# Seven-product matrix blocks run in an interleaved order, with other pauses in two heads

## The chip, the cores and the metric

The kernel runs on one core of a Trainium2 chip. The metric is the device time of one execution in microseconds (us); of several executions the median is given. A profile of one execution records every instruction of the engines: TensorE (PE; PEld is its loading of weights), VectorE (DVE), ScalarE (ACT), GpSimd (POOL) and SyncE (SP), which here only issues DMAs.

## What is computed

Two layers of a bidirectional encoder on a sequence of 512 rows with 2048 features, all in 32-bit floats: an attention layer (16 query heads, 4 key/value heads, rotary positions, gate) and a retention layer (8 heads, forward and backward decay, gate), each followed by a residual sum and a layer norm. Cut to what matters here:

```python
def attention_mixer(h, w_in, q_gain, k_gain, w_out, cos, sin):
    q, k, v, g = jnp.split(h @ w_in, ...)             # 2048 x 5120
    ...
    return (o * jax.nn.silu(g)) @ w_out

def retention_mixer(h, w_in, decay_exp, w_out, cos, sin):
    q, k, v, g = jnp.split(h @ w_in, ...)             # 2048 x 12288
    ...
    o = head_group_norm(fwd + bwd).reshape(B, S, R_V_WIDTH)
    return (o * jax.nn.silu(g)) @ w_out               # 4096 x 2048

def reference(x, ...):
    for i in range(DEPTH):
        y = attention_mixer(x, ...) if i % 2 == 0 else retention_mixer(x, ...)
        x = layer_norm(ALPHA * x + y, ln_gain[i], ln_bias[i])
    return x
```

## The kernel before

**Split products.** Every 32-bit matrix is split into a high and a low part (`split`, L107: a copy by ScalarE, L109, and a subtraction by VectorE, L110), and a product is made of three matmuls: high by high, high by low, low by high (`mm3`, lines 227 to 229). One such group of three is counted as 0.68 us (`MM3`).

**Blocks of seven products.** The input projections of both layers and the output projection of the retention layer's first six heads use a scheme of the Strassen kind: a weight block of 1024 columns is cut in four quarters (`q11`, `q12`, `q21`, `q22`), and seven products of quarter size, numbered 1 to 7, do the work of eight. A product runs over `nc` chunks of weights (four in the layers, two in the pairs); a chunk is 128 x 1024 numbers (512 KB), and for each chunk PE does four groups of three matmuls, two for either half of the rows. Products accumulate in three sets of two PSUM banks, named by `CHAIN`: x takes 1, 6, 7 and 4 one after another, y takes 5 and 3, z takes 2. After each product the two banks are read out by `spill` (L343 copies after 1, 5 and 6; L346 subtracts after 3, L350 after 7, L354 adds after 2; after 4 the consumer reads), and the next product on the same set can't start before that. The eight banks are shared with the heads' scores, values and transposes.

**Where the quarters come from.** `Block.fetch`, `make` and `follow` load a chunk as raw data (SP, L117), add to it in place by an accumulating DMA (POOL, `onto`, L121) or by VectorE (L155 for product 6, L157 for product 4), and split it. A block that is not "first" loads q11 for product 1, adds q12 behind it for product 5, adds q22 (loaded for 6) on VectorE, and q21 (loaded for 2) on VectorE for 4; q22 + q12 makes product 7. A "first" block takes product 2 early: it loads q11 for product 1, q21 for product 2, then q11 again with q12 added for 5, and after 6 adds q21 by DMA. Raw chunks lie in nine buffers (`rp`), which the heads' loads share; split chunks in three (`wp`). The split of a chunk is made two chunks before its use (`AHEAD`), and it needs the `wp` buffer of three chunks earlier.

**Order.** PE's instructions run in the program's order; those of the other engines are placed by a scheduler. The order of products is `ORDER` or, for "first" blocks, `FIRST`:

```python
ORDER = (1, 5, 6, 3, 7, 2, 4)
FIRST = (1, 2, 5, 6, 3, 7, 4)
```

In either layer the blocks 0 and 1 are "first": 1 and 2 of block 0, 1 and 2 of block 1, then 5, 6, 3, 7, 4 of block 0, the same of block 1, then the other blocks in `ORDER` (`in_stream`). The retention output has three pairs of heads; each pair has two blocks of two chunks, the first in `FIRST`, the second in `ORDER` (`out_pair`), and its results are added to a tensor in DRAM (`yD2`). The same lists give the order in which chunks are fetched.

**Heads.** The eight retention heads (`Head.run`) are interleaved with a stream of such products: four score units (`s_unit`, one for each 128 keys), four value units (`o_unit`, each followed by a normalisation on VectorE, POOL and ScalarE, L946 to L950), and transposes of their results (`o_close`, L462). Between them `work.pump(each)` puts `each` us of products into PE's order: 15 units a head, 1.4 us each for heads 0 and 1, which run beside the last input block, and 2.5 us for the others, two of which run beside each pair. `Head.open` loads and splits what head 0 needs.

Of the kernel before, what the change touches and what calls it, by code (L numbers as in the profile page):

```python
# [16 lines left out]
NT = S // P  # L17
# [14 lines left out]
AHEAD = 2  # L32
FETCH = 3
MM3 = 0.68
LOOK = 2
A_KEEP, R_KEEP = 2, 0

PAIRS = 3

ORDER = (1, 5, 6, 3, 7, 2, 4)  # L40
FIRST = (1, 2, 5, 6, 3, 7, 4)
CHAIN = {1: "x", 6: "x", 7: "x", 4: "x", 5: "y", 3: "y", 2: "z"}


# [1 line left out]
def encoder_trunk_kernel(  # L46
# [184 lines left out]
    class Stream:  # L231
# [14 lines left out]
        def until(self, done):  # L246
            while not done():
                self.pump(MM3)

# [64 lines left out]
    def products(blk, op, seq, evacuate):  # L314
        for p in seq:
            ch, fresh = CHAIN[p], p in (1, 5, 2)
            if fresh:
                blk.bk[ch] = [bank() for _ in range(2)]
            for c in range(blk.nc):
                ks = next_chunk()  # L320
                for hook in blk.hooks.get((p, c), ()):
                    hook()
                run_later()
                for j in range(2):
                    k = 2 * c + j
                    for t in range(2):
                        mm3(blk.bk[ch][t], op.st(p, k, t), ks[j], fresh and k == 0, k == 2 * blk.nc - 1, not fresh)
                        yield MM3
            evacuate(blk, p)
# [4 lines left out]
    def spill(deliver):  # L334

        def evacuate(blk, p):
            keep, bk = blk.keep, blk.bk
            for t in range(2):  # L340
                if p in (1, 5, 6):
                    keep[p, t] = temp("t")
                    nc.scalar.copy(keep[p, t], bk[CHAIN[p]][t])  # L343
                elif p == 3:
                    o = keep.pop((6, t))
                    nc.vector.tensor_sub(o, bk["y"][t], o)  # L346
                    deliver(blk, 1, t, o, True)
                elif p == 7:
                    o = keep.pop((5, t))
                    nc.vector.tensor_sub(o, o, bk["x"][t])  # L350
                    deliver(blk, 1, t + 2, o, True)
                elif p == 2:
                    o = keep.pop((1, t))
                    nc.vector.tensor_add(o, bk["z"][t], o)  # L354
                    deliver(blk, 0, t, o, True)
                elif p == 4:
                    deliver(blk, 0, t + 2, bk["x"][t], False)
        return evacuate

    class Sum:  # L360
# [29 lines left out]
        def out_proj(self, og, scale, cols=(0, 1, 2, 3), last=False):  # L390

            for c in cols:
                banks = {}
                for kc in range(2):
                    ks = next_chunk()
                    run_later()
                    for kk in range(2):
                        k = kc * 2 + kk
                        for t in range(NT):
                            if k == 0:  # L400
                                banks[t] = bank()
                            mm3(banks[t], og(k, t), ks[kk], k == 0, k == 3)
                            yield MM3
                for t in range(NT):
# [16 lines left out]
        def out_proj_last(self, og, keep):  # L421
# [3 lines left out]
            for t in range(NT):  # L425
                for c in range(keep, 4):
                    b = bank()
                    for k in range(4):
                        if t == 0 and k % 2 == 0:
                            ws[c, k // 2] = next_chunk()  # L430
                        mm3(b, og(k, t), ws[c, k // 2][k % 2], k == 0, k == 3)
                        yield MM3
                    self.add(t, c, b, 1.0, True)
# [32 lines left out]
    a_in = [Block(a["wa_in"][g], g < 2) for g in range(A_G)]  # L466
    r_in = [Block(a["wr_in"][g], g < 2) for g in range(R_G)]
    a_out = [Plain(a["wa_o"][g], A_KEEP if g == GROUPS - 1 else 4) for g in range(GROUPS)]
    r_pairs = [[Block(a["wr_p"][i, cg], cg == 0, 2) for cg in range(2)] for i in range(PAIRS)]
    r_out = [Plain(a["wr_o"][h], 4 - h * (4 - R_KEEP)) for h in range(2)]  # L470
    for ins, pairs, outs in ((a_in, [], a_out), (r_in, r_pairs, r_out)):
        for b in ins[:2]:
            b.add((1, 2))
        for b in ins[:2]:
            b.add((5, 6, 3, 7, 4))
        for b in chain(ins[2:], *pairs):
            b.add(FIRST if b.first else ORDER)
        for b in outs:
            b.add()

    def in_stream(ins, op, evacuate, n):

        for b in ins[:2]:
            yield from products(b, op, (1, 2), evacuate)
        for b in ins[:2]:
            yield from products(b, op, (5, 6, 3, 7, 4), evacuate)
        for b in ins[2:len(ins) - n]:
            yield from products(b, op, ORDER, evacuate)

    def out_pair(pr, op):  # L490


        def deliver(blk, nb, t, src, own):
            if not own:
                o = temp("c")
                nc.scalar.copy(o, src)
                src = o
            c0 = pr.index(blk) * 1024 + nb * 512
            onto(yD2[:, t, c0:c0 + 512], src)

        for at, n in (((1, 0), 5), ((2, 0), 6), ((5, 0), 3), ((6, 0), 7), ((3, 0), 4)):
            hook(pr[0], *at, op.form, n)
        for b in pr:
            yield from products(b, op, FIRST if b.first else ORDER, spill(deliver))

    FORMS = (((1, 2, 1), (6, 0)), ((1, 2, 3), (6, 1)), ((0, 5, 1), (3, 0)), ((0, 5, 3), (3, 1)),
             ((0, 3, 0), (7, 0)), ((0, 3, 2), (7, 1)), ((0, 7, 0), (4, 0)), ((0, 7, 2), (4, 1)))
# [236 lines left out]
    work = Stream(products(a_in[-1], x1, ORDER, ev1))  # L744
# [4 lines left out]
    for g in range(GROUPS):  # L749
        if g:  # L750
            work = Stream(total.out_proj(groups[g - 1].out, ALPHA if g == 1 else 1.0))
        attention(groups[g], groups[g + 1] if g + 1 < GROUPS else None, work, 2.2 if g else 2.7)
        work.drain()
        if g == 0:
# [11 lines left out]
    de, two, xg, ug, cg, ru, lg, nlg = [const.tile([P, NH], F32, name=n) for n in  # L766
                                        ("de", "two", "xg", "ug", "cg", "ru", "lg", "nlg")]
# [139 lines left out]
    class Head:  # L907
# [54 lines left out]
        def out(self, j, t):  # L962
            return [half(m, t % 2)[:, tcols(j)] for m in self.ogs[t // 2]]

        def open(self):
            self.make_strip()
            self.load_qk()
            self.qk.split(2)
            self.load_v()
            self.v.split(2)  # L970

        def run(self, work, nxt, each):

            for kb in range(NT):
                self.s_unit(kb)
                work.pump(each)
                if kb > 1 and len(self.v.tiles) < 2:
                    self.v.split()
                if kb == 1:
                    self.load_g(0)  # L980
            if nxt:
                nxt.make_strip()
                nxt.load_qk()
            work.pump(each)
            for t in range(NT):
                self.o_unit(t)
                work.pump(each)
                if t == 1:
                    self.load_g(1)
                if t < 2 and nxt:  # L990
                    nxt.qk.split()
                work.pump(each)
                if t:
                    self.o_close(t - 1)
                if t == 2 and self.op:
                    self.op.form(1 + self.h % 2)
            if nxt:
                nxt.load_v()
            work.pump(2 * each)
            self.o_close(NT - 1)  # L1000
# [24 lines left out]
    work = Stream(total.out_proj_last(groups[-1].out, A_KEEP), in_stream(r_in, x2, ev2, 1))  # L1025
# [15 lines left out]
    heads = [Head(h, ops[h // 2] if h < 2 * PAIRS else None) for h in range(R_HEADS)]  # L1041
    total = Sum()
    work = Stream(products(r_in[-1], x2, ORDER, ev2))
    work.pump(17 * MM3)
    heads[0].open()
    work.pump(22.0 * MM3)
    for i in range(PAIRS + 1):
        if i:
            work = Stream(out_pair(r_pairs[i - 1], ops[i - 1]))
# [6 lines left out]
    work = Stream(total.out_proj(heads[-2].out, 1.0))  # L1056
    work.drain()
    work = Stream(total.out_proj_last(heads[-1].out, R_KEEP))
# [88 lines left out]
```

## Time and profile before

| | us |
|---|---|
| median of 3 runs | 2168.99 |
| lowest, highest | 2167.36, 2169.93 |
| the profiled execution | 2166.26 |
| its span, first to last instruction | 2164.4 |

The profile's page gives each engine's busy time, the span in 40 slices, the DMA queues, a chain of work followed back from the end, groups of instructions by line with their count and mean time, and DMA issues with the median time to landing. Other views answer for a stretch of time: waits (who waited for whom: total, times, longest), the order of time of an engine (start, duration, line, tile written and tiles read; in square brackets the idle time before it and what ended it), and busy times by windows (for each engine busy time and count, then the granted PE clock, the DMA engines' busy share and GB/s). The stages follow each other: the attention layer's input blocks (to about 340 us), its heads and output, the retention layer's input blocks (from about 760 us), heads 0 and 1 (about 1600 to 1690 us), the three pairs with heads 2 to 7 (to about 2045 us), and the last output projection and layer norm.

### The profile page before, as it was taken

To read this page: it belongs to the slowest core of one execution; us is meant where nothing else is said; L and a number is where in the kernel's file an instruction comes from. 1 tells how busy PE (TensorE), PEld (TensorE's weight loads), DVE (VectorE), ACT (ScalarE), POOL (GpSimd) and SP (SyncE) were. 2 spreads that over 40 slices of the span, in tenths; PEclk is the share of its full clock that TensorE was granted. 3 is DMA by queue.
4 is the path that set the end of the run, shared out by engine and by line. 5 is a ranking of instruction groups with operands and counts; after the bars stand their busy time and mean duration, and the time that the engine had idled before them with its cause. 6 is when DMAs were issued, how large, how long until landed. Compare 5 with 4: busy or idle time off the path is not lost.

```text
span 2164.4 us, 26442 instructions
## 1 busy us (share of the span) xinstructions
PE 2111.9 (98%) x9744; PEld 1741.5 (80%) x9744; DVE 1599.0 (74%) x2179; ACT 1099.2 (51%) x1453; POOL 382.7 (18%) x455
## 2 busy tenths in 40 slices
PE   8899999999999999999999999999999999999997
PEld 7688888888888878888888888888887878787786
DVE  7887877977767896767786576667687868688666
ACT  5555546654553654444444444444466655565432
POOL 0333332000000122111211111111111212222100
PEclk9999999999999999999999999999999999999999
DMA  9975756563223678686676667558565778878762
GB/s 353 201 183 130 194 155 162 153 221 103 83 78 107 211 179 208 167 252 173 161 230 190 133 168 185 136 149 213 145 168 163 215 171 217 187 186 203 174 203 78
DMA packets 117361, 378.20 MB, mean 175 GB/s; under 512 B 14320, under 2 KB 17392, under 8 KB 117232
## 3 DMA queue, kind: packets, MB, share of 16 engines
q0 software_dynamic: 46432, 152.07, 33.9%
q1 hardware_dynamic: 70368, 223.53, 30.9%
q8 instruction: 76, 1.25, 0.2%
q10 hardware_dynamic: 432, 0.92, 0.1%
q14 instruction: 53, 0.43, 0.1%
HBM read 315.65 MB, written 60.82 MB: 174 GB/s over the span
## 4 chain that ended last, share of the span: by engine, by line
PE 69%; DVE 9%; DMA 9%; issue 8%; ACT 2%; POOL 2%; POOLq 0%; DVEq 0%; ACTq 0%; SPq 0%
PE acc L228 20%; PE acc L227 20%; PE acc L229 20%; DVE wlo L110 3%; DMA raw<-in_wr_p_dram 3%; DMA raw<-in_wr_in_dram 3%; PE tr L462 2%; DMA raw<-in_wa_in_dram 2%; ACT whi L109 1%; PE o L228 1%; PE o L229 1%; PE o L227 1%; DMA q<-qD 1%; DVE f L110 1%; PE s L227 1%
## 5 line engine op out<-in xcount | busy, mean ns | idle before, releaser
L110 DVE TENSOR_TENSOR wlo<-raw,whi 128x1024 fp32r<-128x1024 f32 (+1 forms) x598 | 727.0, 1218 | 371.3 <-ACT whi L109 367.4
L109 ACT CAST whi<-raw 128x1024 fp32r<-128x1024 f32 (+1 forms) x598 | 625.1, 1049 | 675.6 <-PE acc L229 540.3
L227 PE MATMUL acc<-whi,f 128*128 128x512 f32 x2240 | 884.4, 395 | 26.0 <-DVE t L350 14.2
L228 PE MATMUL acc<-wlo,f 128*128 128x512 f32 x2240 | 878.1, 392 | 8.5 <-DVE wlo L110 8.2
L229 PE MATMUL acc<-whi,f 128*128 128x512 f32 x2240 | 876.2, 391 | 0.0
L227 PEld LDWEIGHTS acc<-whi,f 128*128 128x128 f32 x2240 | 422.4, 189 | 116.5 <-ACT whi L109 12.5
L228 PEld LDWEIGHTS acc<-wlo,f 128*128 128x128 f32 x2240 | 422.7, 189 | 102.0 <-DVE wlo L110 17.5
L229 PEld LDWEIGHTS acc<-whi,f 128*128 128x128 f32 x2240 | 422.2, 188 | 88.2
L121 POOL DMA_DIRECT2D raw<-in_wr_in_dram x104 | 90.4, 869 | 406.4 <-DVE wlo L110 227.7
L227 PE MATMUL acc<-whi,ogh 128*128 128x512 f32 x288 | 115.9, 402 | 0.5 <-ACT ogh L109 0.4
L229 PE MATMUL acc<-whi,ogl 128*128 128x512 f32 x288 | 112.8, 392 | 0.0
L228 PE MATMUL acc<-wlo,ogh 128*128 128x512 f32 x288 | 112.6, 391 | 0.0
L343 ACT COPY t<-acc 128x512 f32<-128x512 f32 x138 | 78.8, 587 | 48.7 <-PE acc L229 44.4
L155 DVE TENSOR_TENSOR raw<-raw,raw 128x1024 f32<-128x1024 f32 x80 | 97.7, 1222 | 1.6
L157 DVE TENSOR_TENSOR raw<-raw,raw 128x1024 f32<-128x1024 f32 x58 | 71.0, 1223 | 36.8 <-DMA raw<-in_wr_in_dram 33.0
L445 POOL TENSOR_TENSOR rstd<-rs_e,neg_half 128x1 f32<-128x1 f32 x40 | 29.5, 738 | 365.8 <-DVE rs_e L444 364.8
L673 ACT ACTIVATE p<-s,nmax,q_rs 128x512 f32<-128x512 f32 x64 | 49.9, 779 | 37.5 <-DVE nmax L671 28.8
L110 DVE TENSOR_TENSOR f<-xf,f 128x1024 fp32r<-128x1024 f32 (+2 forms) x52 | 60.0, 1158 | 5.9 <-ACT f L109 5.8
L229 PEld LDWEIGHTS acc<-whi,ogl 128*128 128x128 f32 x288 | 54.1, 188 | 12.2 <-DVE ogl L110 0.4
L445 POOL TENSOR_TENSOR q_rs<-rs_e,neg_half 128x4 f32<-128x4 f32 x16 | 43.4, 2715 | 114.1 <-DVE rs_e L444 114.1
L227 PEld LDWEIGHTS acc<-whi,ogh 128*128 128x128 f32 x288 | 54.3, 188 | 10.7 <-ACT ogh L109 0.8
L121 POOL DMA_DIRECT2D raw<-in_wa_in_dram x48 | 43.3, 938 | 106.4 <-DVE wlo L110 77.8
(175 smaller groups left out, 2383.8 us busy)
## 6 DMA issues: line engine op xcount, KB each, us to landing
raw<-in_wr_in_dram SPq DMA_DIRECT2D x152, 512.0 KB, 4.8
raw<-in_wr_in_dram POOLq DMA_DIRECT2D x104, 512.0 KB, 6.1
raw<-in_wa_in_dram SPq DMA_DIRECT2D x66, 512.0 KB, 5.1
raw<-in_wa_in_dram POOLq DMA_DIRECT2D x48, 512.0 KB, 6.7
raw<-in_wr_p_dram SPq DMA_DIRECT2D x42, 512.0 KB, 5.3
raw<-in_wa_o_dram SPq DMA_DIRECT2D x32, 512.0 KB, 3.5
raw<-in_wr_p_dram POOLq DMA_DIRECT2D x30, 512.0 KB, 8.0
yD<-t POOLq DMA_DIRECT2D x36, 256.0 KB, 6.9
```

Source lines behind the costliest of these rows:

```text
L109: nc.scalar.copy(hi, src)
L110: nc.vector.tensor_sub(lo, src, hi.bitcast(F32))
L121: nc.gpsimd.dma_start(out=x, in_=src, accum_op=ALU.add)
L155: nc.vector.tensor_add(v, v, g[3, c])
L157: nc.vector.tensor_add(v, v, g[2, c])
L227: nc.tensor.matmul(ps, sh, mh, start=start, stop=False, skip_group_check=go_on)
L228: nc.tensor.matmul(ps, sh, ml, start=False, stop=False, skip_group_check=go_on)
L229: nc.tensor.matmul(ps, sl, mh, start=False, stop=stop, skip_group_check=go_on)
L343: nc.scalar.copy(keep[p, t], bk[CHAIN[p]][t])
L445: nc.gpsimd.tensor_tensor(out=dst, in0=e[:, :n], in1=neg_half[:, :n], op=ALU.pow)
L462: nc.tensor.transpose(out=b[:, tcols(i)], in_=src[:, tcols(i)], identity=ident)
L673: nc.scalar.activation(pt, sb, AF.Exp, scale=rs, bias=nmax, accum_out=self.sm[:, h:h + 1])
```

## The change

Two sequences replace `FIRST` and the fixed order of blocks 0, 1 and 2. A pair runs block 0 through 7, then product 1 of block 1, then 4 of block 0, then the rest of block 1. In a layer, product 5 of block 1 goes between 7 and 4 of block 0, and product 1 of block 2 between 7 and 4 of block 1. The blocks of a pair are no longer "first": block 0 keeps product 2's chunks, as in `ORDER`, until product 4. Heads 0 and 1 get factors on their pauses (`THIN`), and `Head.open` loads first and makes its four splits with pauses between them.

```diff
+THIN = (0.4, 1.6, 1.15)
...
 ORDER = (1, 5, 6, 3, 7, 2, 4)
-FIRST = (1, 2, 5, 6, 3, 7, 4)
+
+PAIR_SEQ = ((0, (1, 2, 5, 6, 3, 7)), (1, (1,)), (0, (4,)), (1, (5, 6, 3, 7, 2, 4)))
+LAYER_SEQ = ((0, (1, 2)), (1, (1, 2)), (0, (5, 6, 3, 7)), (1, (5,)), (0, (4,)), (1, (6, 3, 7)), (2, (1,)), (1, (4,)),
+             (2, (5, 6, 3, 7, 2, 4)))
...
-    r_pairs = [[Block(a["wr_p"][i, cg], cg == 0, 2) for cg in range(2)] for i in range(PAIRS)]
+    r_pairs = [[Block(a["wr_p"][i, cg], False, 2) for cg in range(2)] for i in range(PAIRS)]
...
-        for b in ins[:2]:
-            b.add((1, 2))
-        for b in ins[:2]:
-            b.add((5, 6, 3, 7, 4))
-        for b in chain(ins[2:], *pairs):
-            b.add(FIRST if b.first else ORDER)
+        for b, seq in LAYER_SEQ:
+            ins[b].add(seq)
+        for b in ins[3:]:
+            b.add(ORDER)
+        for pr in pairs:
+            for b, seq in PAIR_SEQ:
+                pr[b].add(seq)
...
-        for b in ins[:2]:
-            yield from products(b, op, (1, 2), evacuate)
-        for b in ins[:2]:
-            yield from products(b, op, (5, 6, 3, 7, 4), evacuate)
-        for b in ins[2:len(ins) - n]:
+        for b, seq in LAYER_SEQ:
+            yield from products(ins[b], op, seq, evacuate)
+        for b in ins[3:len(ins) - n]:
             yield from products(b, op, ORDER, evacuate)
...
-        for b in pr:
-            yield from products(b, op, FIRST if b.first else ORDER, spill(deliver))
+        for b, seq in PAIR_SEQ:
+            yield from products(pr[b], op, seq, spill(deliver))
...
-        def open(self):
+        def open(self, work, us):
+
+            self.load_qk()
+            self.load_v()
             self.make_strip()
-            self.load_qk()
-            self.qk.split(2)
-            self.load_v()
-            self.v.split(2)
+            for x in (self.qk, self.qk, self.v, self.v):
+                work.pump(us / 4)
+                x.split()
...
                 self.s_unit(kb)
-                work.pump(each)
+                work.pump(each * (THIN[0] if self.h < 2 and kb < NT - 1 else 1.0))
...
-            work.pump(each)
+            work.pump(each * (THIN[1] if self.h < 2 else 1.0))
             for t in range(NT):
                 self.o_unit(t)
-                work.pump(each)
+                work.pump(each * (THIN[2] if self.h < 2 else 1.0))
...
-                work.pump(each)
+                work.pump(each * (THIN[2] if self.h < 2 else 1.0))
                 if t:
                     self.o_close(t - 1)
...
-    heads[0].open()
-    work.pump(22.0 * MM3)
+    heads[0].open(work, 22.0 * MM3)
```

## The prediction

> **What bounds the kernel now.** I read the page first, its span and the busy shares, then the table of waits of TensorE (PE), whole and by stage, then the order of time around the longest waits.
>
> ```profile
> span 2164.4 us, 26442 instructions
> PE 2111.9 (98%) x9744; PEld 1741.5 (80%) x9744; DVE 1599.0 (74%) x2179; ACT 1099.2 (51%) x1453; POOL 382.7 (18%) x455
> ```
>
> PE works all through: only time in which it stands still, or runs slowly, can be won. The profiled execution took 2166.26 us, 1.9 more than its span and 2.7 less than the median of 2168.99; I make the sum against it and add 2.7 at the end. The waits of PE, each as total, times and longest:
>
> ```profile
> PE acc L227 <- DVE t L350: 14.2, 7, 4.9
> PE acc L227 <- ACT t L343: 3.5, 3, 2.3
> PE tr L462 <- DVE o L950: 3.5, 3, 1.6
> PE o L228 <- DVE inl L110: 0.5, 1, 0.5
> ```
>
> L350 is VectorE's subtraction that empties product 7's banks; product 4 then adds into these banks. Seven waits are as many as there are blocks that run 7 and 4 without another product between: the first two of either layer, and the first of each of three pairs. The same table for 1700 to 2100 us, where the pairs run, and the order of time in PE around the first pair's wait, and the other two:
>
> ```profile
> PE acc L227 <- DVE t L350: 11.0, 3, 4.9
> ...
> 1752.26 0.39 PE L228 MATMUL acc<-wlo,f 128*128 128x512 f32 x1
> 1752.48 0.39 PE L229 MATMUL acc<-whi,f 128*128 128x512 f32 x1
> 1752.72 0.60 PE L462 MATMUL tr<-ident,o 128*128 128x128 f32 x4
> 1758.23 0.67 PE L227 MATMUL acc<-whi,f 128*128 128x512 f32 x1 [4.92 <-DVE t L350]
> ...
> 1877.73 0.71 PE L227 MATMUL acc<-whi,f 128*128 128x512 f32 x1 [3.88 <-DVE t L350]
> ...
> 1999.54 0.47 PE L227 MATMUL acc<-whi,f 128*128 128x512 f32 x1 [2.17 <-DVE t L350]
> ```
>
> A matmul starts 0.22 to 0.23 us after the one before, but its record lasts 0.39, so each wait costs some 0.17 more than the idle time shown: 11.0 + 0.5 = 11.5 us in the pairs and 3.2 + 0.7 = 3.9 in the layers. There is a second cost. Busy time by windows, with PE's granted clock third from the end:
>
> ```profile
> 1758.32:1761.74 3.42, 3.42 (x9) 2.65 (x10) 1.49 (x2) 0.00 (x0) 2.62 (x3) 0.50 0.91 288
> 1877.79:1881.20 3.41, 3.41 (x8) 2.70 (x9) 1.53 (x2) 0.00 (x0) 2.68 (x3) 0.50 0.99 266
> 1987.01:1990.43 3.42, 3.37 (x11) 2.69 (x11) 2.63 (x7) 1.83 (x3) 0.54 (x1) 0.50 0.18 73
> 2000.67:2004.08 3.41, 3.41 (x10) 2.67 (x9) 1.06 (x2) 0.00 (x0) 1.75 (x2) 0.50 0.90 265
> ```
>
> Behind each wait of more than 2.1 us the clock is halved for 3.41 us, which loses half of that: 1.7 us, four times, 6.8 us in all. The third follows another wait (below).
>
> **The change, part by part.** *Pairs: block 1's product 1 between 7 and 4.* It goes to fresh banks, so PE needs no subtraction to go on; its 8 groups of three matmuls take 8 x 3 x 0.227 = 5.4 us, and the subtraction has that long. What is late next is a chunk of weights, split by ScalarE (whi) and VectorE (wlo). VectorE's order of time in the first pair:
>
> ```profile
> 1752.42 0.69 DVE L946 BATCH_NORM_STATS2 o_st<-o 128x6 f32<-128x512 f32 x1
> ...
> 1755.32 0.69 DVE L950 TENSOR_TENSOR o<-o,g 128x512 f32<-128x512 f32 x1 [0.84 <-ACT o L949]
> 1756.26 1.23 DVE L110 TENSOR_TENSOR wlo<-raw,whi 128x1024 fp32r<-128x1024 f32 x1 [0.24 <-ACT whi L109]
> 1757.40 1.28 DVE L350 TENSOR_TENSOR t<-t,acc 128x512 f32<-128x512 f32 x2
> ```
>
> The subtraction waits its turn behind a head's normalisation and behind the split at 1756.26. Chunks are made two ahead, so that split, now of 4's second chunk, will be of product 1's second; it ends at 1757.5, 0.75 us before PE's release at 1758.23. PE wants it one chunk (2.7 us) and one matmul (0.23) after it comes free: it then waits (W - 3.7) us, where W is the wait of today. That is 1.2, 0.2 and nothing for the W of 4.92, 3.88 and 2.17, all below what halved the clock.
>
> *Pairs: chunks kept.* Block 0 no longer loads q11 twice and adds q21 by DMA, but keeps q21's two chunks from product 2 to 4. Per pair two loads (SP) and two accumulating DMAs (POOL) go, and two additions come to VectorE:
>
> ```profile
> L155 DVE TENSOR_TENSOR raw<-raw,raw 128x1024 f32<-128x1024 f32 x80 | 97.7, 1222 | 1.6
> L109 ACT CAST whi<-raw 128x1024 fp32r<-128x1024 f32 (+1 forms) x598 | 625.1, 1049 | 675.6 <-PE acc L229 540.3
> 1690.00:1802.00 112.00, 106.93 (x477) 87.78 (x477) 84.60 (x113) 68.95 (x95) 23.69 (x29) 0.98 0.74 185
> raw<-in_wr_p_dram SPq DMA_DIRECT2D x42, 512.0 KB, 5.3
> raw<-in_wr_p_dram POOLq DMA_DIRECT2D x30, 512.0 KB, 8.0
> ```
>
> Six additions of 1.22 are 7.3 us on an engine with 27 of 112 us idle in a pair (third number with an x in the window's row): they hide there; without that cover 2.4 us a pair would show. They stand ahead of 4's two splits, and I take 0.2 us a pair for that (the bounds are 0 and 2.4). The DMAs that go stood ahead of others. PE's wait at 1986.22, and what it hung on:
>
> ```profile
> 1970.48 0.86 POOL L121 DMA_DIRECT2D raw<-in_wr_p_dram  x1
> 1972.26 0.88 POOL L121 DMA_DIRECT2D raw<-in_wr_p_dram  x1 [0.92 <-DVE wlo L110]
> ...
> 1982.45 1.05 ACT L109 CAST whi<-raw 128x1024 fp32r<-128x1024 f32 x1 [6.78 <-DMA raw<-in_wr_p_dram]
> 1985.60 1.06 ACT L343 COPY t<-acc 128x512 f32<-128x512 f32 x2
> ...
> 1986.22 0.50 PE L227 MATMUL acc<-whi,f 128*128 128x512 f32 x1 [2.29 <-ACT t L343]
> ```
>
> The DMA issued at 1972.26 makes product 7's first chunk (q22 + q12) and lands 10 us later, behind the one issued at 1970.48, which adds q21 and goes. ScalarE sits 6.78 us on it, and the copy of product 6's banks comes late. If it lands in the median of 8.0 us, all behind it moves up by 2.1 and PE's 2.29 is nearly gone; without the two ahead of it I expect more. I count this wait, 2.5 with the 0.17, and half of the other two of its kind (1.2 together), 0.6: 3.1 us, between 0 and 3.8. Product 5 gains too, since its accumulation can now start after product 1's split, four chunks ahead; PE doesn't wait there today, so that counts nothing.
>
> SP's queue keeps its order, since product 4 loads nothing; on POOL's the accumulation that follows block 1's product 1 now stands ahead of 4's stores, and gets one product more before product 5 wants it.
>
> Pairs: 11.5 + 3.1 + 6.8 = 21.4, less 1.4 and 0.6 that come in: **-19.4**.
>
> *Layers.* Product 7 of block 0 is followed by 5 of block 1, then 4 of block 0; 7 of block 1 by 1 of block 2. 3.9 us go. But 5 in these blocks needs a load and an accumulation on top, and now comes one product (10.9 us) sooner, out of busy DMA queues. The issues of the last accumulations for it, PE's end of product 7, and the times to landing (medians of the page; the longest piece of the chain):
>
> ```profile
> 101.81 0.85 POOL L121 DMA_DIRECT2D raw<-in_wa_in_dram  x1 [3.15 <-DVE wlo L110]
> 102.31 0.39 PE L229 MATMUL acc<-whi,f 128*128 128x512 f32 x1
> ...
> 813.37 0.84 POOL L121 DMA_DIRECT2D raw<-in_wr_in_dram  x1 [1.68 <-DMA raw<-in_wr_in_dram]
> 814.54 0.39 PE L229 MATMUL acc<-whi,f 128*128 128x512 f32 x1
> ...
> raw<-in_wr_in_dram POOLq DMA_DIRECT2D x104, 512.0 KB, 6.1
> raw<-in_wa_in_dram POOLq DMA_DIRECT2D x48, 512.0 KB, 6.7
> ...
> 85.49 11.96 DMA raw<-in_wa_in_dram
> ```
>
> These are fourth chunks, wanted 3 x 2.72 = 8.2 us after product 7: at 110.7 and 822.9. With the median landing and 2.3 us of splits (1.05 and 1.22) they are there at 110.8 and 821.8; with 11.96, 5.4 and 4.7 late. Product 4 no longer frees buffers for block 1's product 6 meanwhile, so fewer loads compete: I stay near the medians, 1.2 us for both. Layers: **-2.7**, with 0 to 10 us coming in.
>
> *Heads 0 and 1.* The pauses add up to 15 units per head as before (3 x 0.4 + 1 + 1.6 + 8 x 1.15 + 2); they are short between the scores and longer in the value part. From a value unit to its transposes lie four pauses of 1.4 us: 5.6 becomes 6.4, for the last unit of a head 6.0. Three waits of 3.5 in all (L462 <- L950 above) shrink by 0.84, 0.84 and 0.42, if their chain doesn't move. The values' splits (inl, 0.5) come 1.7 us nearer to the first value unit: I take 0.4 for that. Opening head 0 with the splits spread out has no wait to win. Heads: **-1.7**, from -3.5 to +4 (two such waits at 1.7).
>
> Sum: -19.4 - 2.7 - 1.7 = -23.8; 2166.26 - 23.8 = 2142.5, with 2.7 to the median **2145**.
>
> [...]
>
> **The rivals.** *The engines' chain stays late* (15 in 100). The scheduler may set the subtraction ahead of the split: product 1's second chunk is then 1.28 us later, so PE waits 2.5 and 1.5 us in the first two pairs, the first with a halved clock (1.7); and 7's accumulations land as late as today (3.1 and 1.7 stay). Pairs: 21.4 - 2.5 - 1.5 - 1.7 - 4.8 - 0.6 = 10.3; total -14.7, **2154**. [...] Against: today's order has the split first.
>
> *Product 1 has to wait for banks* (10 in 100). Fresh banks are two of eight; the freest may be that of the head's value unit, emptied by ScalarE just before 1755.32 in the first pair, where PE comes free at 1753.3: 2.0 us and a halved clock, 3.7 in each pair, **2156**. Against: at that place x, the new x, one value bank and one for transposes are in use, five to six of eight.
>
> *Slower: raw buffers run out* (6 in 100). The kept q21 holds two of nine buffers over some ten chunks, and SP's queue is in order. If product 1 of block 1 got its buffer only when PE stands, PE would wait for a load (5.3), two splits (2.3) and the half clock (1.7): 9.3 us a pair, 28 in all, **2173**; it decides from 8 us a pair. Against: by my count the buffers in use never pass eight, with a free one for each load at least three chunks before it is wanted.
>
> That the change doesn't do what it says I exclude: in the new sequences no two neighbours share a bank set.
>
> **How the numbers follow.** Forecast 67 in 100, its own range 2139 to 2151 (all waits gone: -28.8, 2140; layers at +6 instead of -2.7 is outside). With the first two rivals 2139 to 2160 holds over 8 in 10; the third and worse layers lie above. Against the bound of 0.2%, 4.3 us, about what can be told from no change: faster 0.88, same 0.06, slower 0.06.
>
> **What would show it.** No row "acc L227 <- t L350" among PE's waits of 0.3 us or more; a clock of 1.00 in the pairs; waits on whi and wlo of some 1.4 us there; 24 accumulating wr_p issues for 30 and 36 loads for 42; VectorE 7.3 us busier. Waits on banks, or on whi over 2 us at block 1's product 1, would make the forecast wrong.

## The result and the profile after

The whole change takes 2151.89 us (median of 4 runs, 2147.4 to 2153.61) beside 2169.46 for the kernel before in the same runs: a ratio of 0.9915, with a 95% interval of 0.9895 to 0.9935. That is about 18 us less, 14 to 23 by the interval. The forecast was 2145; the result lies 6.9 above it, inside the wide range of 2139 to 2160 and 0.9 above 2151, the upper end of the forecast's own range.

The profiled execution took 2150.57 us. From here on a line number is that of the kernel shown: the change shifts the matmuls to L232 to L234, the splits to L114 and L115, the accumulating DMA to L126, the copy after 1, 5 and 6 to L348, the subtraction after 7 to L355, the addition for product 6 to L160 and the transposes to L467. The page's head and busy row:

```profile
span 2148.8 us, 26395 instructions
...
PE 2108.5 (98%) x9744; PEld 1739.3 (81%) x9744; DVE 1604.8 (75%) x2185; ACT 1100.8 (51%) x1453; POOL 377.2 (18%) x449
```

The waits of PE over the whole span (who waited for whom: total, times, longest):

```profile
PE acc L233 <- DVE wlo L115: 13.3, 16, 2.9
PE acc L232 <- ACT whi L114: 8.1, 4, 6.5
PE o L233 <- DVE inl L115: 3.0, 2, 1.6
...
PE tr L467 <- DVE o L954: 0.4, 1, 0.4
```

No wait on the subtraction (14.2 us in seven places before) and none on the copies (3.5) is left. PE's busy time hardly changes; what went is standing time and time at half clock. What is left of waiting in the stage of the pairs, 1690 to 2100 us, is this:

```profile
PE acc L233 <- DVE wlo L115: 0.8, 1, 0.8
PE acc L232 <- ACT whi L114: 0.4, 1, 0.4
```

The busy times of the same stage (columns as in the prediction, the granted clock third from the end) show PE busy 348.8 of 350 us, at full clock:

```profile
1690.00:2040.00 350.00, 348.81 (x1585) 287.94 (x1584) 287.30 (x392) 212.40 (x288) 76.88 (x96) 1.00 0.77 185
```

The DMA issues and additions of the pairs' weights:

```profile
raw<-in_wr_p_dram SPq DMA_DIRECT2D x36, 512.0 KB, 5.2
...
raw<-in_wr_p_dram POOLq DMA_DIRECT2D x24, 512.0 KB, 7.1
```

```profile
L162 DVE TENSOR_TENSOR raw<-raw,raw 128x1024 f32<-128x1024 f32 x64 | 78.1, 1221 | 38.6 <-DMA raw<-in_wr_in_dram 34.3
```

36 loads for 42, 24 accumulations for 30, and 64 additions for product 4 against 58 before (2185 VectorE instructions for 2179): the six kept-chunk additions, 7.3 us, appear, and cost PE at most the 1.2 us just shown.

**Where the gain was given back.** For each stage I add up what PE loses: the time between the starts of two matmuls, less the 0.227 us that lie between two starts where PE doesn't wait (twenty from 1854.74 to 1859.28 us in the trace of pairs_order), and half of each half-clock stretch (3.41 us at a clock of 0.50).

| stage | lost before | lost after | difference | forecast |
|---|---|---|---|---|
| pairs, to product 4 of the last block | 15.6 + 6.8 clock | 1.6 | -20.8 | -19.4 |
| splits at the end of the third pair (2040 us) | 1.6 | 0 | -1.6 | not counted |
| layers, blocks 0 to 2 | 3.9 | 6.6 + 1.7 clock | +4.4 | -2.7 |
| heads 0 and 1 | 4.6 | 4.0 | -0.6 | -1.7 |
| first attention scores (352 us) | 1.7 | 2.6 + 1.7 clock | +2.6 | not counted |

The sum, -16.0, stands beside 2150.57 - 2166.26 = -15.7. The table takes the places that the argument is about; what it leaves out nearly cancels (waits before 100 us are 1.7 us less, the rest of the attention heads loses 1.0 more).

Two of its numbers belong to these two executions and not to the change. The last row: in heads_only and heads_scores_full (below), whose attention layer is as before, the same place loses 2.5 and 2.4 us and has the halved clock behind it, and in residual_later, which has the whole change there, it loses 1.6 without one. And the 22.4 us that the pairs lost before are at the low end: 2166.26 is below 52 of the 53 other runs on record of the kernel before, and in three traces whose pairs are as before (layers_only, heads_only, heads_scores_full) the same sum gives 25.3, 25.7 and 28.2.

So the pairs give what was forecast or somewhat more, and the layers, which should have given 2.7 more, take 4.4. Two places in the retention layer make most of that. PE's waits from 800 to 890 us, before and after:

```profile
PE acc L227 <- DVE t L350: 0.7, 2, 0.4
```

```profile
PE acc L233 <- DVE wlo L115: 4.7, 2, 2.9
```

VectorE's order of time at the first of them, then at the second, and PE's wait there:

```profile
811.59 2.36 DVE L115 TENSOR_TENSOR wlo<-raw,whi 128x1024 fp32r<-128x1024 f32 x2 [2.19 <-ACT whi L114]
819.22 1.22 DVE L160 TENSOR_TENSOR raw<-raw,raw 128x1024 f32<-128x1024 f32 x1 [5.27 <-DMA raw<-in_wr_in_dram]
820.36 1.22 DVE L115 TENSOR_TENSOR wlo<-raw,whi 128x1024 fp32r<-128x1024 f32 x1
```

```profile
869.34 0.43 DVE L837 TENSOR_SCALAR ln_bias<-ln_bias 128x512 f32<-128x512 f32 x1 [3.52 <-DMA ln_bias<-in_ln_bias_dram]
872.89 0.69 DVE L840 SCALAR_TENSOR_TENSOR res<-res,ln_gain 128x512 f32<-128x512 f32 x1 [3.13 <-DMA res<-nD]
873.50 1.22 DVE L115 TENSOR_TENSOR wlo<-raw,whi 128x1024 fp32r<-128x1024 f32 x1
```

```profile
874.78 0.50 PE L233 MATMUL acc<-wlo,f 128*128 128x512 f32 x1 [2.92 <-DVE wlo L115]
```

At 819 us VectorE has stood for 5.27 us on an addition for product 6, whose load has not landed; the split that PE wants next, of product 5's second chunk, stands behind it and starts only when the addition is through. At 872.89 it is a piece of the residual sum (`residual_2`, hung on product 1 of block 2): its loads are waited for in VectorE's queue, again ahead of a split, that of product 7's last chunk. Block 2's product 1 was moved one product earlier, and the piece went with it.

### The profile page after: what moved, and what is told of

Its sections match the earlier page's. It is cut to its first block, busy times and chain, and to the rows that moved or that the text cites. A ratio compares the mean times of both kernels' runs of the same rounds, so it can differ in the third digit from the quotient of the medians.

```text
span 2148.8 us, 26395 instructions
## 1 busy us (share of the span) xinstructions
PE 2108.5 (98%) x9744; PEld 1739.3 (81%) x9744; DVE 1604.8 (75%) x2185; ACT 1100.8 (51%) x1453; POOL 377.2 (18%) x449
## 4 chain that ended last, share of the span: by engine, by line
PE 74%; DMA 10%; issue 7%; DVE 6%; POOL 2%; ACT 2%; POOLq 0%; SPq 0%; ACTq 0%; DVEq 0%
PE acc L233 21%; PE acc L234 21%; PE acc L232 21%; DMA raw<-in_wa_in_dram 4%; DMA raw<-in_wr_in_dram 3%; PE tr L467 2%; DVE wlo L115 2%; PE o L233 2%; PE o L234 2%; PE o L232 2%; ACT whi L114 1%; PE s L234 1%; PE s L232 1%; PE s L233 1%; DMA q<-qD 1%
## 5 line engine op out<-in xcount | busy, mean ns | idle before, releaser
L115 DVE TENSOR_TENSOR wlo<-raw,whi 128x1024 fp32r<-128x1024 f32 (+1 forms) x598 | 726.4, 1217 | 331.7 <-ACT whi L114 327.1
L114 ACT CAST whi<-raw 128x1024 fp32r<-128x1024 f32 (+1 forms) x598 | 625.3, 1049 | 668.5 <-PE acc L234 537.1
L232 PE MATMUL acc<-whi,f 128*128 128x512 f32 x2240 | 882.9, 394 | 8.2 <-ACT whi L114 8.1
L234 PE MATMUL acc<-whi,f 128*128 128x512 f32 x2240 | 875.2, 391 | 0.0
L232 PEld LDWEIGHTS acc<-whi,f 128*128 128x128 f32 x2240 | 422.1, 188 | 95.2 <-ACT whi L114 9.8
L234 PEld LDWEIGHTS acc<-whi,f 128*128 128x128 f32 x2240 | 421.7, 188 | 88.5
L126 POOL DMA_DIRECT2D raw<-in_wr_in_dram x104 | 90.1, 867 | 391.5 <-DVE wlo L115 238.9
L232 PE MATMUL acc<-whi,ogh 128*128 128x512 f32 x288 | 115.7, 402 | 0.5 <-ACT ogh L114 0.4
L234 PE MATMUL acc<-whi,ogl 128*128 128x512 f32 x288 | 112.7, 391 | 0.0
L162 DVE TENSOR_TENSOR raw<-raw,raw 128x1024 f32<-128x1024 f32 x64 | 78.1, 1221 | 38.6 <-DMA raw<-in_wr_in_dram 34.3
L160 DVE TENSOR_TENSOR raw<-raw,raw 128x1024 f32<-128x1024 f32 x80 | 97.7, 1222 | 10.7 <-DMA raw<-in_wr_in_dram 7.6
L348 ACT COPY t<-acc 128x512 f32<-128x512 f32 x138 | 79.0, 588 | 48.4 <-PE acc L234 44.0
L677 ACT ACTIVATE p<-s,nmax,q_rs 128x512 f32<-128x512 f32 x64 | 49.9, 780 | 36.6 <-DVE nmax L675 28.2
L234 PEld LDWEIGHTS acc<-whi,ogl 128*128 128x128 f32 x288 | 54.0, 188 | 12.2 <-DVE ogl L115 0.4
L115 DVE TENSOR_TENSOR f<-xf,f 128x1024 fp32r<-128x1024 f32 (+2 forms) x52 | 59.9, 1156 | 5.4 <-ACT f L114 5.4
L232 PEld LDWEIGHTS acc<-whi,ogh 128*128 128x128 f32 x288 | 54.2, 188 | 10.8 <-ACT ogh L114 0.8
L126 POOL DMA_DIRECT2D raw<-in_wa_in_dram x48 | 44.2, 956 | 103.7 <-DVE wlo L115 70.0
```

What stands on the lines that cost most here:

```text
L114: nc.scalar.copy(hi, src)
L115: nc.vector.tensor_sub(lo, src, hi.bitcast(F32))
L126: nc.gpsimd.dma_start(out=x, in_=src, accum_op=ALU.add)
L160: nc.vector.tensor_add(v, v, g[3, c])
L162: nc.vector.tensor_add(v, v, g[2, c])
L232: nc.tensor.matmul(ps, sh, mh, start=start, stop=False, skip_group_check=go_on)
```

## The experiments

My theory (A in the expectations) is that the pairs carry the whole gain, the order taking the waits on the subtraction and the kept chunks those on the copies, while the layers' swaps bring splits late and the heads trade one wait for another. Each expectation names its rival (B).

The runs were made in groups, each with its own runs of the kernel before beside it; the table has them all, the groups one after another.

| run | median us (runs) | before, same group | ratio, 95% interval |
|---|---|---|---|
| whole change | 2151.89 (4) | 2169.46 | 0.9915, 0.9895 to 0.9935 |
| pairs_only | 2145.89 (4) | 2170.98 | 0.9882, 0.9867 to 0.9898 |
| layers_only | 2175.03 (12) | 2170.98 | 1.0013, 1.0004 to 1.0022 |
| heads_only | 2171.40 (12) | 2170.98 | 0.9997, 0.9988 to 1.0006 |
| residual_later | 2147.37 (4) | 2170.98 | 0.9886, 0.9872 to 0.9900 |
| pairs_order | 2152.27 (4) | 2172.69 | 0.9906, 0.9890 to 0.9923 |
| pairs_kept | 2161.84 (6) | 2172.69 | 0.9947, 0.9929 to 0.9965 |
| pairs_swap12 | 2147.33 (4) | 2172.69 | 0.9886, 0.9870 to 0.9902 |
| heads_scores_full | 2169.76 (12) | 2172.69 | 0.9992, 0.9983 to 1.0000 |
| pairs_and_heads | 2144.11 (4) | 2172.58 | 0.9876, 0.9862 to 0.9890 |
| pairs_heads_full | 2149.06 (4) | 2172.58 | 0.9896, 0.9882 to 0.9909 |
| pairs_swap01 | 2147.34 (4) | 2172.58 | 0.9889, 0.9875 to 0.9902 |
| pairs_swap01_fetch4 | 2150.77 (5) | 2172.58 | 0.9899, 0.9884 to 0.9913 |

**The three parts alone.** To the kernel before, only the pairs' lines of the diff (`PAIR_SEQ` and the kept chunks):

```diff
+PAIR_SEQ = ((0, (1, 2, 5, 6, 3, 7)), (1, (1,)), (0, (4,)), (1, (5, 6, 3, 7, 2, 4)))
-    r_pairs = [[Block(a["wr_p"][i, cg], cg == 0, 2) for cg in range(2)] for i in range(PAIRS)]
+    r_pairs = [[Block(a["wr_p"][i, cg], False, 2) for cg in range(2)] for i in range(PAIRS)]
```

> Only the pairs' part on top of the kernel before: product 1 of block 1 between 7 and 4, and block 0's chunks kept; layers and heads as before. Theory A, the whole gain comes from here and the layers give some of it back: about 20 us less than before (11.5 of waits on the subtraction, 3 of waits on the copies, 6.8 of halved clock, less 1.5), so about 2149, a little faster than the whole change. Theory B, each part gives something and the losses seen elsewhere are chance: 2155 or more, slower than the whole change (2152).

Only the layers' lines:

```diff
+LAYER_SEQ = ((0, (1, 2)), (1, (1, 2)), (0, (5, 6, 3, 7)), (1, (5,)), (0, (4,)), (1, (6, 3, 7)), (2, (1,)), (1, (4,)),
+             (2, (5, 6, 3, 7, 2, 4)))
```

> Only the layers' part: product 5 of block 1 between 7 and 4 of block 0, product 1 of block 2 between 7 and 4 of block 1. Theory A, from the trace of the whole change: 3.9 us of waits go, but 1.0 and 0.5 in the attention layer, 1.9 and 3.1 in the retention layer and one or two halvings of the clock (1.7 each) come: 2 to 7 us slower than before. Theory B, the forecast: 2.7 us faster, the waits in the whole change being an accident of its timing.

Only the heads' (`THIN` and `Head.open`):

```diff
+THIN = (0.4, 1.6, 1.15)
-    heads[0].open()
-    work.pump(22.0 * MM3)
+    heads[0].open(work, 22.0 * MM3)
```

> Only the other pauses of heads 0 and 1 and the spread opening of head 0. Theory A, from the trace of the whole change, where waits of 5.0 us in the heads became 4.5: within 1 us of before, the waits on the transposes gone and waits of some 3 us on the values' splits (inl) in their place. Theory B, the forecast: 1.7 us faster, no wait on inl over 1 us.

The pairs alone are 1.2% faster, the layers alone 0.04 to 0.22% slower, the heads alone no different. So the pairs carry the whole gain, 22 to 29 us by the interval. In the trace of layers_only PE waits 1.89 at 820 us and 3.44 at 874 us, and the clock is halved for 6.83 us from 872.83. In that of pairs_only, PE's waits from 1700 to 2100 us are a single row:

```profile
PE acc L229 <- DVE wlo L111: 0.3, 1, 0.3
```

**The pairs' two halves.** First the order alone, with the quarters loaded as before; then the kept chunks alone, in the order of before:

```diff
-        for b in pr:
-            yield from products(b, op, FIRST if b.first else ORDER, spill(deliver))
+        for b, seq in PAIR_SEQ:
+            yield from products(pr[b], op, seq, spill(deliver))
```

> Base: the kernel before; only the order of the products in the pairs is changed, block 0 stays "first" (q11 loaded twice, q21 added by DMA). Theory A (the subtraction waits come from the order alone, the copy waits from the extra DMAs): the three waits on the subtraction go (11.5 us) with their three half-clock stretches (5.1), up to 1.4 comes in on splits; the copy wait of 2.29 before block 1 of the third pair, or one on the late chunk of product 7, stays with about 2 to 5 us: 15 less than before, about 2155.5 (2152 to 2158). Theory B (the kept chunks carry the gain, because fewer transfers let ScalarE and VectorE run early): less than 8 us gained, above 2162, with waits on whi or wlo of more than 2 us in the place of the subtraction's.

```diff
-    r_pairs = [[Block(a["wr_p"][i, cg], cg == 0, 2) for cg in range(2)] for i in range(PAIRS)]
+    r_pairs = [[Block(a["wr_p"][i, cg], False, 2) for cg in range(2)] for i in range(PAIRS)]
...
-        for b in pr:
-            yield from products(b, op, FIRST if b.first else ORDER, spill(deliver))
+        for b, seq in zip(pr, (FIRST, ORDER)):
+            yield from products(b, op, seq, spill(deliver))
```

> Base: the kernel before; only the chunks of q21 are kept in the pairs' block 0 (no second load of q11, no accumulation of q21, six additions on VectorE), the order of products stays. Theory A: the three waits on the subtraction after product 7 stay (together 8 to 13 us, two or three half-clock stretches), the waits on the copies (4.0 with the 2.29) go, 0.6 comes in: 3 to 5 us less than before, about 2166.5. Theory B: the subtraction is late because the split ahead of it is late by its DMA; with fewer DMAs these waits fall below 2 us and the gain is 12 or more, below 2159.

PE's waits from 1700 to 2100 us with the order alone, and then with the kept chunks alone:

```profile
PE acc L228 <- ACT t L344: 4.3, 2, 2.2
PE acc L229 <- DVE wlo L111: 1.0, 2, 0.8
PE acc L228 <- ACT whi L110: 0.2, 1, 0.2
```

```profile
PE acc L227 <- DVE t L350: 9.0, 3, 5.1
PE acc L227 <- ACT t L343: 1.4, 1, 1.4
PE acc L227 <- ACT whi L109: 1.3, 1, 1.3
PE acc L228 <- DVE wlo L110: 0.8, 1, 0.8
```

With the order alone the subtraction is gone from the table and the copies (L344, two waits of 2.1 to 2.2 us) stay; with the kept chunks alone the subtraction stays and the waits on copies fall from 3.5 to 1.4. By the waits that is theory A in both. The order alone was worth 20 us (17 to 24 by the interval), more than the expected 15; by the trace's stalls its pairs lose 7.4 instead of 22.4, which is 15. The kept chunks alone were worth 11 (8 to 15), more than the 3 to 5 of theory A and less than the 12 of theory B. A good part of both differences is the execution that the expectations started from: trace against trace (2166.26, 2151.35, 2161.80) the gains are 14.9 and 4.5, and 2166.26 lies 6.4 below the median of the kernel before in this group. With the kept chunks PE's second wait on the subtraction also fell, from 3.88 to 2.08, and with it a half-clock stretch. There VectorE's order differs by one place. A split is done at 1874.52, ahead of the head's multiplication and not behind it, and the subtraction follows at 1876.25:

```profile
1874.52 1.22 DVE L110 TENSOR_TENSOR wlo<-raw,whi 128x1024 fp32r<-128x1024 f32 x1
1875.65 0.69 DVE L953 TENSOR_TENSOR o<-o,g 128x512 f32<-128x512 f32 x1
1876.25 1.28 DVE L350 TENSOR_TENSOR t<-t,acc 128x512 f32<-128x512 f32 x2
```

So one of three waits fell as in theory B: a split took the place in which VectorE idled before (0.84 us, as in the first pair). That place was given by the scheduler; that the fewer DMAs are why it chose so is not shown. The two halves overlap: together they were worth 25 us, not 31, though the lower ends of their intervals, 17 and 8, also add up to 25.

**The layers' parts.** The whole change, with the residual pieces hung on blocks 3 to 6 instead of 2 to 5:

```diff
-            hook(r_in[2 + c], (1, 6, 3, 2)[t], 2, residual_2, c, t)
+            hook(r_in[3 + c], (1, 6, 3, 2)[t], 2, residual_2, c, t)
```

> The whole change, but the residual's loads and sums (residual_2) hang on blocks 3 to 6 of the retention layer in place of 2 to 5. Theory A, the wait of 3.1 us at 874.8 and the halved clock behind it come from VectorE, which stands in its queue for the residual's loads that product 1 of block 2 brought along: both go, 4 to 5 us less than the whole change, 2147. Theory B, the split is late because product 1 itself came earlier: the wait stays, no difference.

Then, on top of the pairs alone, each of the two swaps by itself: product 1 of block 2 between 7 and 4 of block 1 (with the pieces moved), and product 5 of block 1 between 7 and 4 of block 0 (pieces as before):

```diff
+LAYER_SEQ = ((0, (1, 2)), (1, (1, 2)), (0, (5, 6, 3, 7, 4)), (1, (5, 6, 3, 7)), (2, (1,)), (1, (4,)),
+             (2, (5, 6, 3, 7, 2, 4)))
```

> Base: the kernel before, with the pairs' change whole, and of the layers only product 1 of block 2 between 7 and 4 of block 1, the residual pieces hung on blocks 3 and 4 instead of 2 and 3; heads as before. Theory A (of the layers' change the product 5 of block 1 between 7 and 4 of block 0 and the early residual pieces cost, the other swap is clean): the waits on the subtraction at about 161 and 873 us go (1.2 us), those at 104 (2.1) and 817 (0.5) stay, no wait of 1 us or more on splits between 815 and 880; 1 to 3 us less than the pairs alone (2145.9), about 2144.5. Theory B (any such swap in the layers brings the splits late): waits on wlo of 1 us or more between 815 and 880, perhaps with half clock, 2148 to 2152.

```diff
+LAYER_SEQ = ((0, (1, 2)), (1, (1, 2)), (0, (5, 6, 3, 7)), (1, (5,)), (0, (4,)), (1, (6, 3, 7, 4)),
+             (2, (1, 5, 6, 3, 7, 2, 4)))
```

> Base: the kernel before with the pairs' change whole, and of the layers only product 5 of block 1 between 7 and 4 of block 0; residual pieces on blocks 2 to 5 and the other swap as before; heads as before. Theory A (this swap wants product 5's accumulations too soon): the waits on the subtraction at 104 (2.1) and 818 us (0.5) go, those at 161 and 874 (0.7, 0.5) stay; waits on wlo of 0.6 to 1.0 at 111, about 0.6 at 126, and 1.9 to 4.4 in all between 815 and 826, there with VectorE idle for 5 us or more on a DMA; 2146 to 2149, no less than the pairs alone. Theory B (the early residual pieces were the whole cost): no wait over 0.6 between 815 and 826, 2 us less than the pairs alone, 2144.

And the last one with everything fetched a chunk earlier:

```diff
-FETCH = 3
+FETCH = 4
```

> Base: the run before in this list, with loads and accumulations issued four chunks ahead instead of three (FETCH = 4), everywhere. Theory A (product 5's chunks are late because they are issued late): the waits between 815 and 826 fall below 0.5 us in all. Theory B (the DMA queues or the raw buffers set when they land; an issue that stands earlier only waits longer): these waits stay at 1.5 us or more, and the issues' median to landing grows. The time of the whole may move either way, since all stages are fetched differently.

PE's waits from 800 to 890 us in residual_later, and then in pairs_swap12:

```profile
PE acc L233 <- DVE wlo L115: 3.0, 1, 3.0
PE acc L232 <- ACT whi L114: 1.0, 1, 1.0
```

```profile
PE acc L232 <- DVE t L355: 0.4, 1, 0.4
```

With the pieces moved, the wait at 874 us and its half clock are gone in residual_later. But there the waits on product 5 at 819 and 823 us cost 1.17 and 3.23, with 6.83 us at half clock: its layers lose as much as those of the whole change, and its interval and that of the whole change just touch. That the pieces caused the wait at 874 us is shown; what moving them is worth as a whole isn't settled. Swap 1-2 with the pieces moved is clean: from 800 to 890 us one wait of 0.4 on the subtraction is left, and none on a split. Yet it was no faster than the pairs alone; 1.2 us is below what these runs can tell.

Swap 0-1 alone has the wait on product 5 again (2.0 us, and the clock halved behind it), with the same picture in VectorE's order (the wait expected at 111 us did not come, and that at 162 us, on the subtraction, cost 1.8 instead of 0.7):

```profile
817.73 1.23 DVE L160 TENSOR_TENSOR raw<-raw,raw 128x1024 f32<-128x1024 f32 x1 [5.64 <-DMA raw<-in_wr_in_dram]
```

Fetching a chunk earlier did not help: 4.2 us for 2.0, about as long as the two waits together (1.0 and 3.0) in residual_later, which has the same swap and `FETCH` at 3. VectorE stood longer on the same addition:

```profile
819.27 1.23 DVE L160 TENSOR_TENSOR raw<-raw,raw 128x1024 f32<-128x1024 f32 x1 [7.87 <-DMA raw<-in_wr_in_dram]
```

The load that it waits for was issued at 809.64 instead of 810.92 us and landed at 819.18 instead of 817.64. In both runs it is issued within 0.02 us of the end of a split on VectorE, which frees a raw buffer (809.63 and 810.90): the buffers set its issue, and not `FETCH`. That is theory B; that an earlier issue would land no earlier is not shown by it, since 9.54 us to landing against 6.72 is one execution each. Theory B's second sign, a longer median to landing, didn't show (4.5 us for loads against 4.7, 5.9 for accumulations in both): only the stretch around 810 us is slow.

**The rest of the heads.** The kernel before with the longer pauses of the value part but the scores' pauses at 1.0; the pairs with the heads' part whole; and the pairs with the first of these:

```diff
+THIN = (1.0, 1.6, 1.15)
```

> Base: the kernel before; in heads 0 and 1 only the pauses of the value part are longer (1.6 after the scores, 1.15 each), those between the scores stay at 1.0; opening as before. Theory A (the short score pauses bring the first value unit so near to its splits that PE waits on inl): the waits of the transposes on L950 shrink to 0 to 0.6 us in all, waits on inl are 0.7 or less in all; about 3 us less than before, 2167.5. Theory B (the longer pauses of the value part move the values' splits too, or the work that is used up early is missed later): waits on inl of more than 1.5 us, or as much waiting at a later place; no change, 2169.5 to 2171.5.

> Base: the changed kernel without the layers' part (pairs and heads whole, blocks 0 to 2 of the layers as before). Theory A (the layers' part alone gives back what the whole change lacks against the pairs alone): waits as in the pairs alone up to 1600 us, the waits on inl of 1.3 to 1.8 in heads 0 and 1; 2145 to 2147.5 us. Theory B (the heads' part costs once PE runs ahead in the pairs): 2149 or more, with waits or half clock between 1600 and 1700 us that the pairs alone don't have.

> Base: the kernel before with the pairs' change whole, and in heads 0 and 1 only the longer pauses of the value part (1.6 and 1.15), score pauses at 1.0, opening as before. Theory A (the two gains add): the transposes' waits between 1640 and 1690 us fall from 3.6 to under 1 us, one wait on inl of 0.5 to 1.4 stays; about 2.5 us less than the pairs alone (2145.9), 2143.5, below both kernels. Theory B (the work used up earlier is missed later): 2145.5 to 2147, with waits of as much at another place after 1680 us.

PE's waits from 1600 to 1700 us: in heads_only, in heads_scores_full, and in pairs_heads_full:

```profile
PE o L229 <- DVE inl L111: 3.0, 2, 1.6
PE tr L463 <- DVE o L951: 0.2, 1, 0.2
```

```profile
PE o L229 <- DVE inl L111: 1.3, 1, 1.3
PE tr L463 <- DVE o L951: 0.8, 2, 0.6
```

```profile
PE tr L464 <- DVE o L955: 2.2, 2, 1.6
PE o L230 <- DVE inl L112: 1.4, 1, 1.4
```

With the scores' pauses at 1.0 one of the two waits on the values' splits is gone. heads_only also opens head 0 otherwise, but the waits are in head 1, and a second wait there, of 1.6 us, stands in all four traces with the short pauses and in none of the ten without; so it was the short pauses that brought it. The other, 1.3 us, stayed, against theory A: but it is 1.3 also in pairs_swap12, whose heads are as before, and 0.6 in pairs_only, so it differs between executions. The time of heads_scores_full, 2169.76, is at most 0.2% below the kernel before (interval up to 1.0000) and can't be told from it. On top of the pairs the same factors gave nothing: the transposes waited 2.2 us and the time was 2149.06, no better than the pairs alone. The expected 2143.5 was wrong, and why the transposes' waits came back there I did not follow up.

pairs_and_heads, the change without its layers' part, was the fastest of all, 2144.11; its interval lies wholly below that of the whole change. That is theory A: the layers' part is what the whole change gives back. The two ratios put it at about 8 us on top of the pairs, layers_only at 1 to 5 by itself; runs of four leave the first too wide to call these different. Against the pairs alone pairs_and_heads can't be told apart.

## Why the prediction was right, and where it was not

- *Pairs, -19.4*: right in kind, and right in size for the execution that it was worked out from. The trace has -20.8; the runs of the pairs alone have about 25, since in the three other traces with the pairs as before these lose 25 to 28 us and not the 22.4 of that execution. No wait on the subtraction is left, all four half-clock stretches went, and the splits that come in are 1.6 us, in the first pair alone, for 1.4 forecast in the first two. All waits on copies went, where I had counted 3.1 of their 4.0.
- *The split into order and kept chunks* came out as reasoned: the order removes the waits on the subtraction, the kept chunks those on the copies (two of three by themselves, all with the order). Not foreseen was that the kept chunks also shorten one wait on the subtraction.
- *Kept-chunk additions, 0.6*: no more than that; PE stood 0.3 us in the pairs of pairs_only.
- *Layers, -2.7*: the step that failed. Its 3.9 us that go did go; the 1.2 that come in were 8.3. Of these, 3.5 are late splits behind swap 0-1 (1.03 on product 5's fourth chunk and 0.55 on product 6's first in the attention layer, 1.90 on product 5's second in the retention layer), inside the bounds of 0 to 10. Two things were mis-sized there. I took the median landing of 6.1 us for the accumulations: the three issued from 811 to 816 us took 6.0, 8.1 and 8.4. The trace before already had this, for its three accumulations issued from 809 to 814 us took 6.0, 9.5 and 11.6, the last being the very one that I reckoned with. And I took VectorE to be free for the splits, where it stood on an addition for product 6. That addition alone makes the 1.90: the chunk had its high part at 818.56, and a split of 1.22 from there is done at 819.8, where PE wanted it at 819.7. The other 4.8 (3.08 and 1.7 of half clock) I hadn't seen: product 1 of block 2 moves as well, and I counted nothing for it and overlooked the residual pieces hung on it.
- *Heads, -1.7*: the transposes' waits shrank from 3.5 to 0.4, by 3.1 where I had 2.1. The 0.4 for the values' splits was 2.5 (from 0.5 to 3.0): the short pauses between the scores left VectorE too little time to make them. So the two nearly cancel, and 0.6 us is left of 1.7.
- *The opening of the attention heads*: not in the prediction. Here PE gets there 1.7 us sooner than before, waits longer for the splits and has the clock halved behind them (below); traces without the layers' part show the same, so it differs between executions and is no failed step.
- *The total*: that it fell into the range is in part luck. The layers took some 7 us more than forecast, and the pairs gave more than forecast, 25 for 19.4, so that the two errors stand against each other.
- *The rivals*: the engines' chain did not stay late, product 1 of block 1 did not wait for banks, and whatever the pairs' loads waited for raw buffers, PE did not stand for it (busy 348.8 of 350 us). The slower side was in another place than I had put it, the layers, and too small to decide.

## What to carry to other kernels

An interleaving pays where the product put in between needs nothing that is still on its way: product 1 of the next block asks for one load, product 5 for a load and an accumulation. Of a piece of work that is moved, count also what hangs on it, such as hooks with loads of their own: VectorE stood 3.52 and 3.13 us on such loads, and PE waited 3.1 us for the split behind them. Where a trace has the landing of the very DMA that a sum needs, take it and not the median of its kind. And a large gain found in one stage is no reason to apply the same edit in others where the wait was small; there the edit had 3.9 us to win and 8 to lose.

## What the runs showed of the hardware

I had taken each wait of more than 2.1 us to halve PE's clock. The traces of the kernel before and of the whole change show that the place of a wait counts as well. From 20 to 2100 us the clock stands at 0.50 for 3.413 us at a time, from 1758.32, 1877.79, 1987.02 and 2000.67 in the kernel before and from 353.66 and 875.90 in the changed one. These starts are 119.47, 109.23, 13.65 and 522.24 us apart, which are 35, 32, 4 and 153 times 3.413 to within 0.05 us. I laid windows of that length on these starts (20 to 2100 us, some 1,220 windows in the two traces) and worked out for each how long PE stood. I took 0.227 us for a matmul of 512 columns, and as an estimate a half and a quarter of that for 256 and 128. In the six windows that were followed by half clock PE stood 3.32, 3.35, 2.57 and 2.38 us before and 2.71 and 2.42 in the changed kernel; in no other did it stand more than 2.05, be it in one wait or several. A matmul at half clock starts 0.43 us after the one before (six from 354.19 to 356.75 in the changed kernel) and is counted at 0.227 here too. One window of either kind in the changed kernel, each with the window after it (columns as before, the clock third from the end):

```profile
350.24:353.66 3.42, 1.41 (x5) 0.42 (x3) 3.42 (x6) 1.86 (x3) 0.00 (x0) 1.00 0.33 90
353.66:357.07 3.41, 3.41 (x8) 2.74 (x9) 2.39 (x4) 0.91 (x1) 0.00 (x0) 0.50 0.25 63
1671.20:1674.61 3.41, 1.66 (x6) 1.05 (x6) 3.41 (x6) 3.38 (x6) 0.00 (x0) 1.00 0.73 243
1674.61:1678.02 3.41, 2.54 (x11) 2.13 (x12) 3.23 (x5) 3.04 (x7) 0.00 (x0) 1.00 0.66 210
```

In the first PE stood 2.71 us in several pieces, the longest wait 1.31, and the clock halved; in the third 2.05, and it did not, though waits of 1.36 and 1.61 us end at 1672.21 and 1675.48: the third ends within the second of them. The kernel before has two waits on the subtraction of nearly one length. That of 1.97 us, which ends at 104.66, began 0.2 us ahead of its window (102.86 to 106.27), in which PE stood 1.89, and the window after it ran at 1.00; that of 2.17, which ends at 1999.54, lies whole in one (1997.26 to 2000.67) in which PE stood 2.38, and the one after it ran at 0.50. So in these traces a wait of about 2 us cost 1.7 more or nothing, by how much standing fell into the same window.
